# Modulation sums on TensorE in fewer, longer groups: a two-layer diffusion trunk on one core

## Chip, cores and metric

The kernel runs on one core of a Trainium2 chip. The metric is device time in microseconds (us): the median of several runs of the program. A lower number is better. The profile is one more execution of the same program, recorded by the hardware profiler.

## What is computed

A trunk of two layers works on 512 latent tokens and 256 context tokens of width 1024. Every layer normalises its input and modulates it: six rows of 1024 numbers (shift, scale and gate, for attention and for the MLP) come from a product of a conditioning vector with a 1024 x 6144 weight matrix. Latent tokens have the vector `c`, context tokens the vector `c_ctx`. Three attention groups (windowed, neighbourhood and latent) read one input projection; an output projection and a squared-ReLU MLP of width 4096 follow. The core of the reference:

```python
def modulate(h, shift, scale):
    return h * (1 + scale) + shift
...
    silu_c = jax.nn.silu(c)
    silu_cc = jax.nn.silu(c_ctx)
...
        mod_x = jnp.split((silu_c @ w_ada[l] + b_ada[l])[:, None, :], N_MOD, axis=-1)
        mod_c = jnp.split(silu_cc @ w_ada[l] + b_ada[l], N_MOD, axis=-1)
...
        hx = modulate(rmsnorm(x, norm1_g[l]), mod_x[0], mod_x[1])
        hc = modulate(rmsnorm(ctx, norm1_g[l]), mod_c[0], mod_c[1])
...
        x = x + mod_x[5] * sq_relu_mlp(modulate(rmsnorm(x, norm2_g[l]), mod_x[3], mod_x[4]),
...
```

Everything is in float32. The kernel keeps that accuracy in its large products by splitting each operand into a high and a low part and adding three products (high by high, low by high, high by low).

## The kernel before

**Work and staging.** The program is written as one pass over two layers: modulation, norm, input projection, attention groups B, A and C in turn, output projection, MLP. Weights come from memory in tiles of 128 x 1024 (tag `raw`, four buffers), and are split into `wh` and `wl` (L449 on ScalarE, L450 on VectorE). TensorE multiplies 128-row weight tiles with 384 or 512 token columns: L466 to L468 in the input projections, L603 and L652 to L661 in attention (scores, transposes, values), L693 to L695 in the output projection, L1075 to L1077 and L1109 to L1111 in the MLP. PSUM tiles have tags of their own: `psd` (two buffers), `pss` (three), `pst` (two), `psv` and `psa` (one each).

**What orders the work.** All engines run their own instruction list in order. Which list that is, the tile framework's scheduler decides when the program is built (`schedule_with_timeline_sim=True`): it simulates a timeline and, among the instructions that are ready, takes the one of highest priority, which by default is the one that stands earlier in the code. A block under `tc.high_priority()` stands ahead of all that. So the order on the engines differs from that of the code, and a change of priorities moves instructions in it.

**The modulation rows.** The first two rows of the first layer come in four quarters (`ada_quarter`), as the first thing in the program. Rows 2 to 4 of the first layer are made on TensorE while its attention runs (`ada_row`): eight blocks of 128 weight rows are loaded one by one (L209, on SP's queue, 512 KB each, to a `raw` tile), and each block has four matmuls (L211), one for each quarter of the 1024 features. The stationary operand is `ct`, 32 columns wide, so that the four quarters go to four column strips of the array (`tile_position`). They add up in the one `psa` tile:

```python
            for j in range(4):
                T.matmul(ps[32 * j:32 * j + 32, :256], ct[:, k, :], raw[:, j * 256:(j + 1) * 256],
                         start=(k == 0), stop=(k == KC - 1), tile_position=(0, 32 * j))
```

Row 5 of the first layer and all six of the second are made on VectorE while the MLP of the first layer holds TensorE (`ada_dve`, a generator that `step` in the MLP advances by one block at a time). For each block of weight rows (L269, 256 KB, tag `tm`) VectorE multiplies by the vector's entries and adds up (L275); an accumulator has 128 x 512 numbers, and there are four for a row (two halves of the features, two vectors), or two where the last layer needs only the latent vector. What is left is a sum over the 128 partitions: a matmul with a tile of ones for each accumulator, again 32 columns wide and on strips of their own (L280). Then, for a gate, VectorE adds the bias and the row goes to memory (L289 to L291); for a shift or a scale VectorE copies it (L297) and four transposes on TensorE (L300) bring it to columns.

**Names that follow.** Lines with a number, as L211, are those of the kernel before. A matmul in float32 is recorded as two passes, so that an "x2" in the trace's timeline is one matmul. The broad matmuls, whose operands are of the type fp32r, and the transposes are recorded as one pass. "Stop" below means a run of L211 or of L280 matmuls between two broad ones.

Of the kernel before, what the change touches and what calls it, by code (L numbers as in the profile page):

```python
# [26 lines left out]
RD = D ** -0.5  # exact: 1 / 32  # L27
# [3 lines left out]
STEPS = 2  # L31
STEP5 = 3
# [45 lines left out]
def hybrid_dit_kernel(  # L78
# [38 lines left out]
    def raw_tile(shape):  # L117
        return view(sbuf(1024, F32, "raw"), shape)
# [42 lines left out]
    def fence(t_, key):  # L161
        """holds the load of a tile back until another load of the start has come, so that the loads
        keep the order in which they are needed"""
        if FENCE.get(key, -1) in fences:
            V.tensor_copy(t_[:, 0:1], fences[FENCE[key]][:, 0:1])
# [24 lines left out]
    # silu of the two conditioning vectors (columns 0 and 1 of each chunk)  # L190
# [12 lines left out]
    def ada_row(l, m):  # L203
        """one of the six modulation rows of both conditioning vectors: column tile j holds
        the features j * 256 .. j * 256 + 255 on partitions 32 j (c) and 32 j + 1 (c_ctx)"""
        ps = ps_a()
        for k in range(KC):
            raw = raw_tile([D])
            nc.sync.dma_start(raw, w_ada[l, k * P:(k + 1) * P, m * D:(m + 1) * D])  # L209
            for j in range(4):  # L210
                T.matmul(ps[32 * j:32 * j + 32, :256], ct[:, k, :], raw[:, j * 256:(j + 1) * 256],  # L211
                         start=(k == 0), stop=(k == KC - 1), tile_position=(0, 32 * j))
# [22 lines left out]
    # the first shift and scale come by quarters of the features, to let the products start early  # L235
# [23 lines left out]
    def ada_dve(l, ms):  # L259
        """modulation rows on the vector engine, while the products hold the tensor engine;  # L260
        the sum over partitions is a product with ones"""
        for m in ms:
# [14 lines left out]
            # column tile j: the sums of half j % 2 for conditioning vector j // 2  # L277
            ps = ps_d()
            for j in range(2 * nw):
                T.matmul(ps[32 * j:32 * j + 32, :], ones, acc[j // 2][j % 2], start=True, stop=True,  # L280
                         tile_position=(0, 32 * j))
# [35 lines left out]
    def pump(n):  # L317
        """the first layer's rows are spread over its attention"""
        calls[0] += n
        if n and calls[0] in ADAPOS:  # L320
            pump_until(0, 2 + ADAPOS.index(calls[0]))
# [13 lines left out]
    # shift and 1+scale folded with the norm's gain, as per-partition columns  # L335
# [21 lines left out]
    def rstat_x(ss, n):  # L357
        """rows' halves of the mean square -> 1 / root of their sum + EPS"""
        r = small(n, "rst", 4)
        v_ = ss.rearrange("p (i h) -> p i h", h=2)  # L360
        V.scalar_tensor_tensor(r, v_[:, :, 0], EPS, v_[:, :, 1], ALU.add, ALU.add)
        G.tensor_tensor(r, r, mhalf[:, 0:n], ALU.pow)
        return r
# [25 lines left out]
    def norm_T(groups, l, which, pre=None):  # L389
        """normalised, modulated input, feature-major, as hi + lo"""  # L390
# [85 lines left out]
    def feat_pair(l, h, ws, ntoks):  # L476
        """two chunks at once, so that each feature block of the input is used as it comes"""
# [14 lines left out]
        else:  # L492
            # the first half of the tokens while the norm of the second is under way
# [18 lines left out]
    def rope(t_, rows, tab, mask):  # L512
        """in place on the latent tokens of a feature-major page"""
# [23 lines left out]
    def stack_q(t_, n):  # L537
        """two heads of a chunk -> per head one page holding hi and lo on its two halves"""
# [8 lines left out]
    def dup_k(t_, n):  # L547
        """two heads of a chunk -> per head (hi, hi) and (lo, lo)"""
# [35 lines left out]
    def att_unit(kind, rows, vap, put, sinkcols=None):  # L584
        """rows: four of dict(passes=[(lhsT, rhs)], segs=[(c0, n, mask)]), two per column half.
        vap(kb, half) -> values [128 keys, 64]; put(pv) stores the unit's output."""
# [42 lines left out]
        # key blocks: token tile -> column of the row's probabilities  # L629
# [85 lines left out]
    for l in range(DEPTH):  # L715
# [138 lines left out]
        # C: low-rank queries, keys/values and the shared rope key, token-major  # L854
# [37 lines left out]
        # the scores' scale goes with the gain of the query's norm  # L892
# [49 lines left out]
        def up_q(c):  # L942
            """one chunk of 128 features of the queries"""
# [12 lines left out]
        # the rope parts of all four heads  # L956
# [20 lines left out]
        def split_heads(res, n_all, rope_hl, name):  # L977
            """the two heads of a chunk to pages of 96 rows, 64 of the chunk and 32 of the rope part"""
# [249 lines left out]
def _layout(inp):  # L1228
# [15 lines left out]
    # relative position bias of a query in a 16-column block against the keys of three column blocks  # L1244
# [12 lines left out]
    def heads_apart(w, n):  # L1257
        """columns of the first n of every head, then those of the rest of every head"""
        w = w.reshape(L, w.shape[1], 4, -1)
        return np.concatenate([w[..., :n].reshape(L, w.shape[1], -1), w[..., n:].reshape(L, w.shape[1], -1)], axis=-1)  # L1260
# [29 lines left out]
```

## Time and profile before

| | us |
|---|---|
| the three runs | 1683.29, 1682.86, 1677.75 |
| their median | 1682.86 |
| span of the profiled execution | 1677.7 |
| TensorE (PE) busy in it, 8994 matmul passes | 1630.2 (97%) |
| VectorE (DVE) busy | 1012.7 (60%) |
| ScalarE (ACT) busy | 683.4 (41%) |
| GpSimd (POOL) busy | 606.3 (36%) |
| DMA queue of SP, share of 16 engines | 31.9% |
| mean granted TensorE clock | 0.990 |

The span runs from the first to the last instruction; the profiled execution is at the lower end of the three runs. Busy is the time in which an engine had an instruction in work; for TensorE that includes the time that matmuls overlap in its pipeline, so that a busy stretch can still hold time that another order of the same matmuls wouldn't need. The granted clock is a share of 2.4 GHz: 1.00 is that level, 0.50 the lower one of 1.2 GHz.

### The profile page before, as it was taken

What the parts mean: (1) busy time and instruction counts of PE and PEld (TensorE: products, weight loads), DVE (VectorE), ACT (ScalarE), POOL (GpSimd) and SP (SyncE); (2) the same over time, 40 slices, a digit from 0 to 9 for tenths busy, and PEclk for the clock granted to TensorE, in tenths of its full rate; (3) what the DMA queues carried; (4) which work ended last, traced back from release to release, by engine and by line L of the source; (5) the groups of instructions that cost most, each with busy time, mean ns of one, the idle gap of its engine ahead of it and who ended that gap; (6) DMA issues with size and microseconds to landing.
All of it is one profiled execution on the core that took longest, in us unless ns stands there. A gap on an engine that the chain in (4) does not pass through costs nothing.

```text
span 1677.7 us, 24080 instructions
## 1 busy us (share of the span) xinstructions
PE 1630.2 (97%) x8994; PEld 1354.9 (81%) x8994; DVE 1012.7 (60%) x1995; ACT 683.4 (41%) x1342; POOL 606.3 (36%) x564
## 2 busy tenths in 40 slices
PE   6999999999999999999999999999999899999997
PEld 3887788776798988889889879878776788888886
DVE  3555666687787667444454686686777633444346
ACT  5544466656631212212122245446755532222232
POOL 1111543553433342333424341144443323333335
PEclk8999999999999999999999999999999999999999
DMA  9545311220154423333333442222120233332332
GB/s 311 157 140 161 111 47 36 67 63 15 32 182 126 129 85 119 103 105 130 94 107 107 145 151 62 65 56 59 42 79 17 63 89 100 101 97 92 100 100 76
DMA packets 156421, 164.46 MB, mean 98 GB/s; under 512 B 8960, under 2 KB 111368, under 8 KB 156304
## 3 DMA queue, kind: packets, MB, share of 16 engines
q1 hardware_dynamic: 156304, 162.92, 31.9%
q8 instruction: 71, 1.16, 0.3%
q14 instruction: 46, 0.38, 0.1%
HBM read 155.53 MB, written 2.12 MB: 94 GB/s over the span
## 4 chain that ended last, share of the span: by engine, by line
PE 90%; DVE 5%; DMA 2%; ACT 1%; issue 1%; POOL 1%; SPq 0%; POOLq 0%; DVEq 0%; ACTq 0%
PE psd L1075 9%; PE psd L1076 9%; PE psd L1077 8%; PE psv L661 5%; PE pss L603 5%; PE pst L652 5%; PE pss L1109 3%; PE pss L1111 3%; PE pss L1110 3%; PE psd L466 3%; PE psd L468 3%; PE psd L467 3%; PE psa L1110 2%; PE psa L1111 2%; PE psd L693 2%; PE pst L1109 2%
## 5 line engine op out<-in xcount | busy, mean ns | idle before, releaser
L450 DVE TENSOR_TENSOR wl<-raw,wh 128x1024 fp32r<-128x1024 f32 (+1 forms) x168 | 220.7, 1315 | 197.6 <-issue 89.9
L712 POOL TENSOR_TENSOR xlat<-xlat,rtmp 128x512 f32<-128x512 f32 x159 | 236.1, 1509 | 280.7 <-DVE rtmp L711 273.6
L449 ACT CAST wh<-raw 128x1024 fp32r<-128x1024 f32 (+1 forms) x168 | 174.6, 1040 | 315.3 <-PE pst L1111 179.8
L1075 PE MATMUL psd<-hT,wh 128*128 128x384 f32 (+2 forms) x752 | 265.5, 353 | 3.9 <-DVE hT L413 3.9
L1076 PE MATMUL psd<-hT,wl 128*128 128x384 f32 (+2 forms) x752 | 264.9, 352 | 2.5 <-DVE wl L450 2.5
L1077 PE MATMUL psd<-hT,wh 128*128 128x384 f32 (+2 forms) x752 | 266.1, 354 | 0.2 <-POOL hT L415 0.2
L627 POOL TENSOR_TENSOR prob<-prob,sm 128x512 f32<-128x512 f32 (+3 forms) x110 | 126.4, 1157 | 258.5 <-DVE sm L620 211.8
L1084 POOL TENSOR_TENSOR relu<-relu 128x384 f32<-128x384 f32 (+1 forms) x96 | 98.2, 1024 | 319.2 <-ACT uh L1083 288.0
L1082 ACT ACTIVATE relu<-psd 128x384 f32<-128x384 f32 (+1 forms) x93 | 49.1, 528 | 283.7 <-PE psd L1077 280.6
L619 ACT ACTIVATE prob<-prob,m 128x513 f32<-128x513 f32 (+6 forms) x160 | 121.0, 756 | 99.2 <-DVE m L614 69.7
L1075 PEld LDWEIGHTS psd<-hT,wh 128*128 128x128 f32 x752 | 142.0, 189 | 15.8 <-DVE hT L413 4.4
L1076 PEld LDWEIGHTS psd<-hT,wl 128*128 128x128 f32 x752 | 141.9, 189 | 12.8 <-DVE wl L450 3.2
L1077 PEld LDWEIGHTS psd<-hT,wh 128*128 128x128 f32 x752 | 141.9, 189 | 10.9 <-issue 0.8
L1085 DVE TENSOR_TENSOR ul<-relu,uh 128x384 fp32r<-128x384 f32 (+1 forms) x96 | 59.1, 617 | 142.7 <-POOL relu L1084 142.6
L275 DVE SCALAR_TENSOR_TENSOR acc<-araw,consts,acc 128x512 f32<-128x512 f32 x140 | 114.3, 842 | 13.6 <-DMA araw<-in_w_ada_dram 12.9
L652 PEld LDWEIGHTS pst<-consts,prob 128*128 128x128 f32 x688 | 77.5, 140 | 49.6 <-issue 38.5
L652 PE MATMUL pst<-consts,prob 128*128 128x128 f32 x688 | 114.7, 282 | 2.3 <-POOL prob L627 1.3
L466 PE MATMUL psd<-hT,wh 128*128 128x384 f32 (+1 forms) x280 | 97.6, 349 | 0.5 <-DVE rtmp L711 0.2
L468 PE MATMUL psd<-hT,wl 128*128 128x384 f32 (+1 forms) x280 | 97.0, 346 | 1.1 <-DVE wl L450 1.1
L467 PE MATMUL psd<-hT,wh 128*128 128x384 f32 (+1 forms) x280 | 96.9, 346 | 0.0
L656 ACT COPY pT<-pst 128x512 f32<-128x512 f32 x124 | 70.9, 584 | 63.6 <-PE pst L652 63.3
L1111 PE MATMUL pss<-wh,ul 128*128 128x512 f32 x224 | 87.4, 390 | 0.0
(265 smaller groups left out, 3586.6 us busy)
## 6 DMA issues: line engine op xcount, KB each, us to landing
raw<-in_w_mlp_in_dram SPq DMA_DIRECT2D x64, 512.0 KB, 4.0
raw<-in_w_mlp_out_dram SPq DMA_DIRECT2D x64, 512.0 KB, 4.1
araw<-in_w_ada_dram SPq DMA_DIRECT2D x112, 256.0 KB, 4.7
raw<-in_w_in_dram SPq DMA_DIRECT2D x24, 512.0 KB, 4.2
raw<-in_w_ada_dram SPq DMA_DIRECT2D x24, 512.0 KB, 4.8
raw<-in_w_ada_dram SPq DMA_DIRECT2D x32, 256.0 KB, 5.6
raw<-in_w_out_dram SPq DMA_DIRECT2D x8, 512.0 KB, 5.5
raw<-in_w_out_dram SPq DMA_DIRECT2D x16, 256.0 KB, 3.5
```

Source lines behind the costliest of these rows:

```text
L449: A.copy(hi, raw)
L450: V.tensor_tensor(lo, raw, bc(hi), ALU.subtract)
L466: T.matmul(ps[:, :n], wh[:, k, :], hh[k][:, s0:s0 + n], start=(k == 0), stop=False)
L467: T.matmul(ps[:, :n], wh[:, k, :], hl[k][:, s0:s0 + n], start=False, stop=False)
L468: T.matmul(ps[:, :n], wl[:, k, :], hh[k][:, s0:s0 + n], start=False, stop=(k == KC - 1))
L627: G.tensor_tensor(p_[:, :w_], p_[:, :w_], sm.to_broadcast([P, w_]), ALU.mult)
L652: T.transpose(pt[:, r * P:(r + 1) * P], pts[r][:, pos[r][kb]:pos[r][kb] + P], ident)
L712: (V if fast and (RLAST if fast == "end" and t == 3 else RFAST)[dh] == "V" else G).tensor_tensor(xt[t][:, cs], xt[t][:, cs], tmp, ALU.add)
L1075: T.matmul(o_, wh[:, k, :], hh[k][:, sl], start=(k == 0), stop=False)
L1076: T.matmul(o_, wl[:, k, :], hh[k][:, sl], start=False, stop=False)
L1077: T.matmul(o_, wh[:, k, :], hl[k][:, sl], start=False, stop=(k == KC - 1))
L1111: T.matmul(a_, ul[:, ts_], wh[:, c % 2, :], start=False, stop=fin)
```

## The change

Two places are edited. In `ada_row` the loop takes the blocks of weight rows in pairs (`ADAB = 2`): both are loaded to `raw` tiles, and then the eight matmuls of the pair are issued together under high priority, those of the block loaded second first. The flags `start` and `stop`, which open and close the sum in PSUM, move with that order. In `ada_dve` the two or four sums of a row are issued under high priority too, in falling order of `j`. The number and the shapes of all instructions stay as they are. The other hunks of the diff take out comments and move line numbers by seven or eight: L211 becomes L218, L280 L288, L300 L308, L269 L276, L446 L454, L1075 to L1077 L1083 to L1085, L1109 to L1111 L1117 to L1119.

```diff
--- before.py
+++ after.py
@@ -24,11 +24,12 @@
 D_FF = 4096
 KC = D // P
 EPS = 1e-6
-RD = D ** -0.5  # exact: 1 / 32
+RD = D ** -0.5
 BIG = 1e30
 HUGE = 3e38
 PS = {"d": 2, "s": 3, "t": 2, "v": 1, "a": 1}
 STEPS = 2
+ADAB = 2
 STEP5 = 3
 PREP1 = 1
 PT = {"A": "A", "B": "AV", "C": "AV"}
@@ -201,15 +202,21 @@
     gdram = {}
 
     def ada_row(l, m):
-        """one of the six modulation rows of both conditioning vectors: column tile j holds
-        the features j * 256 .. j * 256 + 255 on partitions 32 j (c) and 32 j + 1 (c_ctx)"""
+
+
         ps = ps_a()
-        for k in range(KC):
-            raw = raw_tile([D])
-            nc.sync.dma_start(raw, w_ada[l, k * P:(k + 1) * P, m * D:(m + 1) * D])
-            for j in range(4):
-                T.matmul(ps[32 * j:32 * j + 32, :256], ct[:, k, :], raw[:, j * 256:(j + 1) * 256],
-                         start=(k == 0), stop=(k == KC - 1), tile_position=(0, 32 * j))
+        for k0 in range(0, KC, ADAB):
+            raws = []
+            for k in range(k0, k0 + ADAB):
+                raws.append(raw_tile([D]))
+                nc.sync.dma_start(raws[-1], w_ada[l, k * P:(k + 1) * P, m * D:(m + 1) * D])
+
+
+            with tc.high_priority():
+                for k in reversed(range(k0, k0 + ADAB)):
+                    for j in range(4):
+                        T.matmul(ps[32 * j:32 * j + 32, :256], ct[:, k, :], raws[k - k0][:, j * 256:(j + 1) * 256],
+                                 start=(k == ADAB - 1), stop=(k == KC - ADAB), tile_position=(0, 32 * j))
         if m in (2, 5):
             br = rtemp(256, name="brow")
             nc.sync.dma_start(br, brow[l, m])
@@ -274,11 +281,12 @@
                         else:
                             V.scalar_tensor_tensor(a_, raw, ct[:, k, w:w + 1], a_, ALU.mult, ALU.add)
                     yield
-            # column tile j: the sums of half j % 2 for conditioning vector j // 2
+
             ps = ps_d()
-            for j in range(2 * nw):
-                T.matmul(ps[32 * j:32 * j + 32, :], ones, acc[j // 2][j % 2], start=True, stop=True,
-                         tile_position=(0, 32 * j))
+            with tc.high_priority():
+                for j in reversed(range(2 * nw)):
+                    T.matmul(ps[32 * j:32 * j + 32, :], ones, acc[j // 2][j % 2], start=True, stop=True,
+                             tile_position=(0, 32 * j))
             rows = slice(0, 64 * nw)
             if m in (2, 5):
                 gd = dp.tile([2, D], F32, name=f"gate{l}_{m}")
```

The instruction lists differ on TensorE from the first layer's attention on, up to the end of its MLP; in the second layer they are the same after its first products. Three places show how.

In the attention of the first layer, within the second of `ada_row`'s three rows, TensorE's list of before reads (row number, line, operation, tile out<-in, shape of the moving operand, count; a modulation matmul shows as 32x256):

```order
548 L211 MATMUL psa<-raw,consts 32x256 x3
549 L661 MATMUL psv<-pT,vtok 64x256 x4
550 L652 MATMUL pst<-consts,prob 128x128 x4
551 L211 MATMUL psa<-raw,consts 32x256
552 L652 MATMUL pst<-consts,prob 128x128 x4
553 L603 MATMUL pss<-kh,qs 128x256
554 L603 MATMUL pss<-kl,qs 128x256
555 L571 MATMUL psd<-consts,qkraw 128x128
556 L211 MATMUL psa<-raw,consts 32x256 x3
557 L603 MATMUL pss<-kh,qs 128x256
558 L603 MATMUL pss<-kl,qs 128x256
559 L211 MATMUL psa<-raw,consts 32x256 x2
```

In the list of after a stop of the same modulation row reads:

```order
515 L476 MATMUL psd<-hT_126,wl 128x384
516 L474 MATMUL psd<-hT_128,wh 128x384
517 L475 MATMUL psd<-hT_129,wh 128x384
518 L476 MATMUL psd<-hT_128,wl 128x384
519 L474 MATMUL psd<-hT_130,wh 128x384
520 L218 MATMUL psa<-raw,consts 32x256 x8
521 L611 MATMUL pss<-kh,qs 128x256
522 L611 MATMUL pss<-kl,qs 128x256
523 L611 MATMUL pss<-kh,qs 128x256
```

Before, the matmuls of a block are taken apart by whatever was ready at the time, into stops of three, one, three and two. Now eight stand together, here between an input projection and scores.

In the first layer's MLP, the sums of the second layer's second row stand directly ahead of the four transposes of their result in the list of before (the first of the row's four sums stands alone, 66 rows further up):

```order
2839 L1109 MATMUL pst<-wh,uh 128x512
2840 L1110 MATMUL pst<-wl,uh 128x512
2841 L1111 MATMUL pst<-wh,ul 128x512
2842 L280 MATMUL psd<-acc,ones 32x512 x3
2843 L300 MATMUL psd<-consts,arow 128x128 x4
2844 L1075 MATMUL psd<-hT_4952,wh 128x384
2845 L1076 MATMUL psd<-hT_4952,wl 128x384
```

In the list of after the four sums stand 77 rows ahead of the transposes, within the products of another accumulation:

```order
2735 L1117 MATMUL pst<-wh,uh 128x512
2736 L288 MATMUL psd<-acc,ones 32x512 x4
2737 L1118 MATMUL pst<-wl,uh 128x512
2738 L1119 MATMUL pst<-wh,ul 128x512
2739 L1117 MATMUL pst<-wh,uh 128x512
...
2811 L1118 MATMUL pst<-wl,uh 128x512
2812 L1119 MATMUL pst<-wh,ul 128x512
2813 L308 MATMUL psd<-consts,arow 128x128 x4
2814 L1083 MATMUL psd<-hT_4952,wh 128x384
2815 L1084 MATMUL psd<-hT_4952,wl 128x384
```

Between those two places there are now 76 rows of MLP matmuls; before there were none.

On SP, whose list is its queue of loads, the end of the first layer's MLP read before (L446 from `w_in` are weights of the next input projections, L269 the weight rows for the modulation):

```order
186 L1122 DMA raw<-in_w_mlp_out_dram 128x2x512
187 L269 DMA araw<-in_w_ada_dram 128x512
188 L1122 DMA raw<-in_w_mlp_out_dram 128x2x512
189 L446 DMA raw<-in_w_in_dram 128x8x128 x5
190 L269 DMA araw<-in_w_ada_dram 128x512
191 L446 DMA raw<-in_w_in_dram 128x8x128
192 L269 DMA araw<-in_w_ada_dram 128x512 x15
193 L288 DMA arow<-in_b_ada_dram 32x512 x2
```

and reads now:

```order
183 L276 DMA araw<-in_w_ada_dram 128x512 x5
184 L1130 DMA raw<-in_w_mlp_out_dram 128x2x512 x2
185 L454 DMA raw<-in_w_in_dram 128x8x128 x3
186 L276 DMA araw<-in_w_ada_dram 128x512 x8
187 L454 DMA raw<-in_w_in_dram 128x8x128
188 L276 DMA araw<-in_w_ada_dram 128x512 x8
189 L454 DMA raw<-in_w_in_dram 128x8x128
190 L296 DMA arow<-in_b_ada_dram 32x512 x2
```

Of the last row's 16 modulation loads, one stood behind five of these weight loads and 15 behind six; they are now in two groups of eight behind three and four of them.

## Rows read from the trace of the kernel before

**Rows 1.** The page's part 4: the chain that ended last, by engine.

```profile
PE 90%; DVE 5%; DMA 2%; ACT 1%; issue 1%; POOL 1%; SPq 0%; POOLq 0%; DVEq 0%; ACTq 0%
```

**Rows 2.** Windows: stretch, length, busy PE PEld DVE ACT POOL, clock, DMA share, GB/s.

```profile
58.50:262.00 203.50, 202.56 (x1332) 162.01 (x1331) 131.66 (x369) 100.18 (x220) 60.83 (x81) 1.00 0.39 115
438.00:999.00 561.00, 557.39 (x2791) 493.33 (x2792) 335.07 (x446) 148.93 (x251) 207.41 (x165) 0.99 0.37 118
```

**Rows 3.** Timeline of TensorE, 75 us: start, length, line, [idle before <-releaser].

```profile
75.31 0.33 PE L467 MATMUL psd<-hT,wh 128*128 128x384 f32 x1
75.49 0.34 PE L468 MATMUL psd<-hT,wl 128*128 128x384 f32 x1
75.75 0.62 PE L211 MATMUL psa<-raw,consts 128*32 128x256 f32 x2
...
76.59 0.34 PE L467 MATMUL psd<-hT,wh 128*128 128x384 f32 x1
```

**Rows 4.** Timeline of TensorE, 67 us: six modulation matmuls in one stop.

```profile
67.20 0.34 PE L468 MATMUL psd<-hT,wl 128*128 128x384 f32 x1
67.47 1.06 PE L211 MATMUL psa<-raw,consts 128*32 128x256 f32 x12
...
68.68 0.28 PE L603 MATMUL pss<-kl,qs 128*128 128x256 f32 x1
```

**Rows 5.** Timeline of TensorE, 510 us: two sums in one stop.

```profile
510.11 0.34 PE L1076 MATMUL psd<-hT,wl 128*128 128x384 f32 x1
510.37 1.05 PE L280 MATMUL psd<-acc,ones 128*32 128x512 f32 x4
...
511.64 0.40 PE L1110 MATMUL pss<-wl,uh 128*128 128x512 f32 x1
```

**Rows 6.** Groups by line and shape, TensorE: passes | busy, mean ns | idle.

```profile
L211 PE MATMUL psa<-raw,consts 128*32 128x256 f32 x192 | 21.0, 390 | 0.4 <-DMA raw<-in_w_ada_dram 0.4
...
L280 PE MATMUL psd<-acc,ones 128*32 128x512 f32 x40 | 15.7, 605 | 0.0
```

**Rows 7.** Timeline at 686 us: TensorE and VectorE, three sums and their transposes.

```profile
685.66 1.06 PE L280 MATMUL psd<-acc,ones 128*32 128x512 f32 x6
685.70 2.32 DVE L450 TENSOR_TENSOR wl<-raw,wh 128x1024 fp32r<-128x1024 f32 x1
...
688.68 0.99 PE L300 MATMUL psd<-consts,arow 128*128 128x128 f32 x4 [1.95 <-DVE arow L297]
```

**Rows 8.** Windows, as in rows 2, of the stretch behind that.

```profile
688.70:692.30 3.60, 3.60 (x13) 3.60 (x14) 3.20 (x6) 0.00 (x0) 3.10 (x3) 0.53 0.70 245
```

**Rows 9.** Timeline of SP at 178 us: two loads of modulation weights.

```profile
178.08 0.34 SPq L209 DMA_DIRECT2D raw<-in_w_ada_dram  x1
...
178.53 0.37 SPq L209 DMA_DIRECT2D raw<-in_w_ada_dram  x1
```

**Rows 10.** Timeline of TensorE, 182 to 186 us: the stops that use them.

```profile
182.07 0.64 PE L211 MATMUL psa<-raw,consts 128*32 128x256 f32 x8 [0.16 <-DMA raw<-in_w_ada_dram]
...
184.49 0.64 PE L211 MATMUL psa<-raw,consts 128*32 128x256 f32 x8 [0.19 <-DMA raw<-in_w_ada_dram]
```

**Rows 11.** Line L209: its loads, from issue to landing.

```profile
DMA to landing us min/median/max: 3.6/4.8/6.7
```

**Rows 12.** Timeline of VectorE: accumulations and idle time of the last rows.

```profile
774.57 0.74 DVE L275 SCALAR_TENSOR_TENSOR acc<-araw,consts,acc 128x512 f32<-128x512 f32 x1
...
953.44 1.22 DVE L450 TENSOR_TENSOR wl<-raw,wh 128x1024 fp32r<-128x1024 f32 x1 [7.51 <-issue]
...
958.14 1.37 DVE L711 TENSOR_TENSOR rtmp<-pss,gates 128x512 f32<-128x512 f32 x2 [3.48 <-PE pss L1111]
...
985.51 0.73 DVE L275 SCALAR_TENSOR_TENSOR acc<-araw,consts,acc 128x512 f32<-128x512 f32 x1
```

**Rows 13.** Timeline of SP, 936 to 990 us: loads at the layer's end.

```profile
939.65 15.41 SPq L446 DMA_DIRECT2D raw<-in_w_in_dram  x5
...
964.23 8.65 SPq L269 DMA_DIRECT2D araw<-in_w_ada_dram  x15
```

## The prediction

> **What bounds the kernel now.** I read the page first: 90% of the chain that ended last is TensorE [rows 1]. Then the busy time by stage: in the first layer's attention (58.5 to 262 us) TensorE is busy for 202.6 of 203.5 us, in its MLP (438 to 999) for 557.4 of 561.0; no other engine passes 65% in either [rows 2]. So a step that TensorE doesn't have to make there is worth its whole length, and the word busy must be looked into: the timeline shows what it hides.
>
> Broad matmuls follow each other start to start in 0.18 us for 384 columns [rows 3], so about 0.12 for 256 columns, in proportion. A modulation matmul, which fills only 32 of the array's 128 columns, breaks that beat. One alone (x2, since each runs as two passes): from the broad matmul before it (75.49) to the second after it (76.59) are 1.10 us where two steps would be 0.36. The stop costs 0.74 us, of which 0.62 show as its own busy time and 0.12 as switching [rows 3]. Four of them, one block of weight rows, are busy for 0.64 (the x8 of [rows 10]): no longer than one. Six of them: 68.68 - 67.20 = 1.48, less 0.18 and 0.12, is 1.18 us, 1.06 of it busy [rows 4]. The price is that of a stop with one round of up to four matmuls, and some 0.43 more for a second round. The sums over partitions behave alike: two in one stop cost 511.64 - 510.11 = 1.53, less 0.36, is 1.17 us, 1.05 of it busy [rows 5].
>
> **The change, part by part.**
>
> *Modulation rows (L211).* The order of before has 30 such stops for 96 matmuls: 26 of one to four, three of five to seven, one of ten. Their busy time in sum is 21.0 us [rows 6]. The order of after has 12 stops of eight. Eight are two rounds, as six are: 1.06 us busy, 12.7 in sum, so 8.3 us less busy, and 18 switches of 0.12 fewer, 2.2. Together, 10.5, is the upper end; 8.3 is the lower, since eight of the old stops lie directly before a value product (L661), which is itself 64 columns wide and pays for a switch in any case. I take 9.0, nearer to the lower, because more than a quarter of the stops share their switch.
>
> *Sums (L280).* Before: 15 stops, 15.7 us busy [rows 6]. After: seven, three of four matmuls and four of two, each one round of 1.05 us: 7.4. Saved are 8.3 busy and eight switches of 0.12: 9.3 us. Three matmuls in one stop took 1.06 [rows 7], so a fourth adds next to nothing. The order of their four places is turned round, which no row shows; if turned places did not overlap, three stops would each take three passes of 0.43 more, 4 us in all, and if they overlap as before, nothing. I take nothing, which the rows in rising order are nearest to.
>
> *The stall at 686.7.* In the second layer's second row the last three sums are followed at once by the four transposes of their result (L300). These wait for VectorE, which first finishes a weight split of 2.32 us and then copies the result: TensorE idles 1.95 us [rows 7]. In the next 3.6 us the granted clock is 0.53, that is mostly the lower level, 1.2 GHz, and 13 matmuls fill it [rows 8]; nine at 0.18 and four narrower ones at 0.12 or less are some 2.0 us at 2.4 GHz, so 1.6 are lost. In the order of after these sums stand 77 rows ahead of their transposes, some 17 us of MLP matmuls, which cover split and copy. Saved 3.5 us; if that cover failed, nothing. No other stop of after has its transposes right behind it.
>
> *Added: waits for loads.* A stop of eight begins with the block that was loaded second, so it waits for both, and what stands behind it in TensorE's queue waits too. Mostly the weight tiles of the stop before are what comes free: in six of the nine follow-up stops both loads are issued after that stop (0.7 us after its start, the second 0.45 later), in three only one is. Before, loads issued at 178.08 and 178.53 [rows 9] were waited for until 182.07 and 184.49 [rows 10]: 4.0 and 6.0 us. So start to start 7.1 us are needed for two, 5 to 6 for one. The steps of the rows that the order of after puts between stops sum to 7.2, 7.7, 7.5, 5.8, 6.8 and 8.2 us for the six (the short ones in the third modulation row), and 6.1 to 6.2 for the three. Shortfall 1.3 + 0.3 = 1.6 us; none at the lower end, 8 at the upper (rival 1).
>
> The Trainium skill has a price for a load (DMA: Bandwidth & Descriptors, section Anatomy of one DMA): about 2.0 us fixed plus the bytes at 436 GB/s, fitted on another issue path than this kernel's. By it two blocks of 512 KB would take an estimated 4.4 us, no stop would wait, and the sum would be 1.6 us lower. The rows of this trace are longer, and I go by them.
>
> *Added: waits for sums.* Each of the seven stops now waits for all of VectorE's accumulations of its row. In five these ended before the time of the new place. In the second layer's third row the place was 774.9 us and the last accumulation ends at 775.3 [rows 12]: 0.5 us with its signal, taken. In its last row the order moves the stop 142 rows forward, to what was 971.3, while the accumulations ended at 986.2 [rows 12]. But it moves these as well: VectorE idled for 7.5 and 3.5 us before 953.4 and 958.1 [rows 12], because the loads of this row stood in SP's queue behind five weight loads issued over 15.4 us and came out only at 964.23 [rows 13]. After, eight of them stand behind three of those. Sixteen accumulations of 0.73 us fit into that idle time and the 8 us behind it. Cost 0, from -1 (a lighter VectorE at the layer's end) to 15, if the loads still come at 964.
>
> *Else.* The weight loads of the next projections follow the shorter modulation rows earlier on SP; the value products keep their 131 stops; the second layer's order is the same after its first products. All 0, and hidden behind a TensorE that has no gaps there.
>
> *Sum* against this execution's own 1677.7: - 9.0 - 9.3 - 3.5 + 1.6 + 0.5 = 1658.0. The three runs shown have their lowest at this time and their median at 1682.9, 5.2 above. A repeated measurement may fall on either level; by the other it is 1682.9 - 19.7 = 1663.2. I take about the middle, **1660 us**, against a median of 1682.9.
>
> **The rivals.**
> 1. *The loads come late.* If every block takes the 6.7 us of the slowest of this line [rows 11], the stops with two loads need 7.85 us (shortfalls 0.6, 0.2, 0.4, 2.0, 1.1: 4.3) and those with one 7.4 (1.3, 1.2, 1.3: 3.8). That is 8.1 us, and the one that idles 2 us pulls 1.6 of half clock behind it as in [rows 8]: 9.7, or 8 more than the sum has, 1668. For it: two loads side by side do slow each other. Against: the middle of this line is 4.8 [rows 11].
> 2. *Slower.* The same place, with longer loads: each stop that idles about 2 us costs 3.6 with the half clock after it. Nine are 32 us more than a sum without the 1.6: 1690. It is slower than before from seven such stops on, for which loads would have to take 8 us and more, beyond any seen here. The Trainium skill says of matmuls (TensorE: Matmul & The Clock Gate, section The mechanism) that they start and end strictly in order; by that rule nothing behind a waiting stop covers for it, and the trace agrees, with 0.16 and 0.19 us of idle ahead of such stops.
> 3. *The last row's sums come too early.* TensorE waits up to 15 us for them at the layer's end, and half clock follows: 1676. For it: VectorE idled while these loads were held back. Against: SP's queue is freed.
> 4. *The time goes into other waits.* A reordered attention stage gives back what it saved, where the softmax steps on VectorE and ScalarE pace it: 1680, no change. Against it: 0.9 us of idle in 203 [rows 2].
>
> **How the numbers follow.** Forecast 0.70 (1652 to 1667), rival 1 0.12, rival 3 0.05, rival 4 0.08, rival 2 0.05. A measurement of this kernel can tell about 0.3%, 5 us. Faster is below 1677.8, where forecast, rival 1 and rival 3 lie: 0.87; the same, rival 4: 0.08; slower 0.05. The low end takes the upper savings and no wait from the lower level (1654) and a lighter layer's end, 1652; the high end takes in rival 1 on the upper level, 1672.
>
> **What would show it.** Right: 12 modulation stops of x16 with about 1.06 us busy each, seven of sums; about 12.7 and 7.4 us busy in sum; full clock around the transposes of the second layer's second row; the first attention stage shorter by about 7 us, the MLP by about 12. Wrong: a load named before the modulation stops with several us, TensorE idle before the last sums, or another fall of the clock. All of it rests on a stop's price being the switch and not its matmuls: if four sums in one stop take 2 us, the second term falls.

## The result, and the profile after

The changed kernel takes 1664.45 us (median of four runs) beside 1682.38 for the kernel before: 17.9 us less. The ratio, taken over the runs and not from the medians, is 0.9899 with a 95% interval of 0.9879 to 0.9919, that is 17 us less (20 to 14). On another chip the two medians were 1664.70 and 1681.44, a ratio of 0.9902 (0.9886 to 0.9919). One of the four runs came out at 1998.74 us under a lower clock and is left out of the ratio. The forecast was 1660, the range 1652 to 1672.

The page of the changed kernel (part 1, then part 4 by engine) says little by itself. TensorE has 15.2 us less to do; it is busy for 97% of the span as before, and has 89% of the chain that ended last, against 90 [rows 1]:

```profile
PE 1615.0 (97%) x8994; PEld 1354.3 (81%) x8994; DVE 1010.4 (61%) x1995; ACT 684.2 (41%) x1342; POOL 610.5 (37%) x564
...
PE 89%; DVE 6%; DMA 2%; ACT 1%; issue 1%; POOL 0%; SPq 0%; POOLq 0%; DVEq 0%; ACTq 0%
```

The groups by line and shape answer to [rows 6]. The same 192 and 40 passes are busy for 12.8 and 7.4 us where they took 21.0 and 15.7; the waits for loads grew from 0.4 to 1.6:

```profile
L218 PE MATMUL psa<-raw,consts 128*32 128x256 f32 x192 | 12.8, 385 | 1.6 <-DMA raw<-in_w_ada_dram 1.6
...
L288 PE MATMUL psd<-acc,ones 128*32 128x512 f32 x40 | 7.4, 605 | 0.0
```

TensorE's timeline shows one stop of each kind (start, length, line). For the eight modulation matmuls, 141.44 - 139.95 less one step of 384 and one of 256 columns is 1.20 us, hardly more than the six of [rows 4]. For four sums, 657.93 - 656.28 less two steps of 512 columns (0.227 each) is 1.20 us, as for two in [rows 5]:

```profile
139.95 0.34 PE L474 MATMUL psd<-hT,wh 128*128 128x384 f32 x1
140.22 1.07 PE L218 MATMUL psa<-raw,consts 128*32 128x256 f32 x16
141.22 0.39 PE L611 MATMUL pss<-kh,qs 128*128 128x256 f32 x1
141.44 0.28 PE L611 MATMUL pss<-kl,qs 128*128 128x256 f32 x1
...
656.28 0.39 PE L1117 MATMUL pst<-wh,uh 128*128 128x512 f32 x1
656.60 1.06 PE L288 MATMUL psd<-acc,ones 128*32 128x512 f32 x8
657.60 0.50 PE L1118 MATMUL pst<-wl,uh 128*128 128x512 f32 x1
657.93 0.39 PE L1119 MATMUL pst<-wh,ul 128*128 128x512 f32 x1
```

Where the time went is read best from the starts of the same broad matmul in both timelines. The table is worked out from them: by how much the changed kernel is ahead, at a time of the kernel before.

| at (us of before) | ahead (us) | what lies in between |
|---|---|---|
| 60 | -0.6 | start of the program, not changed |
| 340 | 6.4 | modulation rows: +7 |
| 400 | 5.1 | half clock behind an idle time at 360 that is in both: -1.2 |
| 490 | 5.7 | clock at the start of the MLP: +0.6 |
| 600 | 10.4 | sums: four stops fewer by 1.18, +4.7 |
| 720 | 15.1 | one stop, the stall and the half clock at 688: +4.7 |
| 790 | 14.6 | one stop less, a new wait of 1.7: -0.5 |
| 1010 | 16.6 | two stops fewer by 1.18, small waits and transposes: +2.0 |
| 1300 and on | 15.3 | half clock near 1240, in both, of other cost: -1.3 |

Of the 19.7 us that the sum had, 15 are there in these two executions. The first attention stage is 7.0 us shorter and the MLP 10.9, where the prediction named about 7 and 12.

### The profile page after: what moved, and what is told of

Read it like the earlier page. It is cut to its first block, busy times and chain, and to the rows that moved or that the text cites. A ratio compares the mean times of both kernels' runs of the same rounds, so it can differ in the third digit from the quotient of the medians.

```text
span 1662.8 us, 24078 instructions
## 1 busy us (share of the span) xinstructions
PE 1615.0 (97%) x8994; PEld 1354.3 (81%) x8994; DVE 1010.4 (61%) x1995; ACT 684.2 (41%) x1342; POOL 610.5 (37%) x564
## 4 chain that ended last, share of the span: by engine, by line
PE 89%; DVE 6%; DMA 2%; ACT 1%; issue 1%; POOL 0%; SPq 0%; POOLq 0%; DVEq 0%; ACTq 0%
PE psd L1083 9%; PE psd L1084 9%; PE psd L1085 9%; PE psv L669 5%; PE pss L611 5%; PE pst L660 5%; PE pss L1117 3%; PE pss L1118 3%; PE pss L1119 3%; PE psd L474 3%; PE psd L475 3%; PE psd L476 3%; PE pst L1119 2%; PE pst L1118 2%; PE psv L1118 2%; PE psv L1119 2%
## 5 line engine op out<-in xcount | busy, mean ns | idle before, releaser
L457 ACT CAST wh<-raw 128x1024 fp32r<-128x1024 f32 (+1 forms) x168 | 174.8, 1041 | 301.1 <-PE pst L1119 175.4
L1083 PE MATMUL psd<-hT,wh 128*128 128x384 f32 (+2 forms) x752 | 264.8, 353 | 3.9 <-DVE hT L421 3.9
L1085 PE MATMUL psd<-hT,wh 128*128 128x384 f32 (+2 forms) x752 | 265.2, 353 | 0.1
L1090 ACT ACTIVATE relu<-psd 128x384 f32<-128x384 f32 (+1 forms) x93 | 49.1, 528 | 279.4 <-PE psd L1085 276.4
L1083 PEld LDWEIGHTS psd<-hT,wh 128*128 128x128 f32 x752 | 141.4, 188 | 15.7 <-DVE hT L421 4.4
L1084 PEld LDWEIGHTS psd<-hT,wl 128*128 128x128 f32 x752 | 141.4, 188 | 12.8 <-DVE wl L458 3.2
L1085 PEld LDWEIGHTS psd<-hT,wh 128*128 128x128 f32 x752 | 141.3, 188 | 9.7 <-DVE hT L423 0.3
L282 DVE SCALAR_TENSOR_TENSOR acc<-araw,consts,acc 128x512 f32<-128x512 f32 x140 | 116.9, 860 | 15.0 <-DMA araw<-in_w_ada_dram 14.0
L1118 PE MATMUL pss<-wl,uh 128*128 128x512 f32 x224 | 87.4, 390 | 0.0
```

What stands on the lines that cost most here:

```text
L457: A.copy(hi, raw)
L1083: T.matmul(o_, wh[:, k, :], hh[k][:, sl], start=(k == 0), stop=False)
L1084: T.matmul(o_, wl[:, k, :], hh[k][:, sl], start=False, stop=False)
L1085: T.matmul(o_, wh[:, k, :], hl[k][:, sl], start=False, stop=(k == KC - 1))
L1118: T.matmul(a_, uh[:, ts_], wl[:, c % 2, :], start=False, stop=False)
```

## Experiments

Line numbers are those of each run's own kernel: L287, L288 and L282 are the sums, L212, L217 and L218 the modulation matmuls. The kernel before had a median of 1682.38 us beside after; beside the runs below, made in three groups on three chips, it had 1680.31 (rows alone, sums alone, both loops rising, one strip after the other), 1679.56 (without priority, four blocks, quarters) and 1681.44 (the pair run together at the end). Ratios are to the kernel before of the same group, and a difference of 2 to 3 us between medians of two groups need not come from the edit.

**One part at a time.** Two kernels with one half of the diff each. The orders of TensorE divide cleanly: the first has the attention of after and the MLP of before, the second the reverse.

> Only the modulation rows (L218) are changed; the sums are issued as before. The order has 12 stops of eight modulation matmuls and the 15 sum stops of before, three of them directly ahead of their transposes. Theory (the price is paid per stop, and the two parts add up): about 7 us less than the kernel before, from the first layer's attention alone; the MLP of the first layer as long as before, with the idle time of about 2 us ahead of the transposes at 686 us still there. Rival (the gain comes from the sums alone, the waits of the pairs eat what the rows save): within 2 us of the kernel before.

> Only the sums (L280) are changed; the modulation rows are issued as before. The order has the 30 modulation stops of before and the seven sum stops of after. Theory: about 11 us less than the kernel before (8 stops by 1.18 us are 9.4, the idle time of 2.0 and the half clock of 1.6 behind it, less 1.7 for six MLP matmuls that now come ahead of their weight split, and 0.3 for transposes in two places), all of it between 500 and 1000 us. Rival (the idle time goes elsewhere, only stops are saved): about 8 us.

Rows alone: 1673.0 us, 0.9962 of before (0.9949 to 0.9975). Sums alone: 1671.96, 0.9953 (0.9941 to 0.9965). The two gains by medians, 7.3 and 8.4, add up to 15.7, close to the 16.7 and 17.9 of both. The 8.4 alone would fit the rival of sums alone (8) about as well as the theory (11); what speaks for the theory is the timeline. The groups by line show each gain in its own place, first rows alone, then sums alone:

```profile
L287 PE MATMUL psd<-acc,ones 128*32 128x512 f32 x40 | 15.7, 605 | 0.0
L218 PE MATMUL psa<-raw,consts 128*32 128x256 f32 x192 | 12.8, 385 | 1.6 <-DMA raw<-in_w_ada_dram 1.6
```

```profile
L212 PE MATMUL psa<-raw,consts 128*32 128x256 f32 x192 | 21.0, 390 | 0.6 <-DMA raw<-in_w_ada_dram 0.5
L282 PE MATMUL psd<-acc,ones 128*32 128x512 f32 x40 | 7.4, 605 | 0.0
```

With sums alone the run is 10.9 us ahead of before at 1010 us, as expected, and 8.6 at the end: two stretches of half clock in the second layer, whose order is the same, took the rest. With rows alone the stall ahead of the transposes is still there, but the clock does not fall behind it. The timeline row and the window (columns as in [rows 2]) of rows alone stand against [rows 7, 8]:

```profile
681.27 0.66 PE L307 MATMUL psd<-consts,arow 128*128 128x128 f32 x4 [1.95 <-DVE arow L304]
...
682.00:685.60 3.60, 3.60 (x23) 3.60 (x22) 2.51 (x5) 0.00 (x0) 2.42 (x2) 1.00 0.80 275
```

**What makes the stops long: the direction of the loops or the priority.** First the loops of after count up:

```diff
-                for k in reversed(range(k0, k0 + ADAB)):
+                for k in range(k0, k0 + ADAB):
...
-                                 start=(k == ADAB - 1), stop=(k == KC - ADAB), tile_position=(0, 32 * j))
+                                 start=(k == 0), stop=(k == KC - 1), tile_position=(0, 32 * j))
...
-                for j in reversed(range(2 * nw)):
+                for j in range(2 * nw):
```

> After, with both loops counting up instead of down (block loaded first, j = 0 first), still under high priority and with both loads ahead. The order now has 24 modulation stops of four and 17 sum stops, 14 of them of one matmul. Theory (the falling order is what makes the stops long, since all of a group then wait for the last operand; the price is per stop): rows 24 by 0.74 = 17.8 instead of 12 by 1.20 = 14.4 us, less 1.9 of waits for loads; sums 10 more stops by 1.18 = 11.8 us; in all 13 us slower than after, about 1677. Rival (high priority or the pairs of loads bring the gain, the direction of the loops doesn't matter): within 2 us of after, 1664.

1679.55 us, 0.9997 of before (0.9987 to 1.0007): the whole gain is gone, with the priority and the paired loads still in place. Only the cover of the stall stays: TensorE has no idle time ahead of L308. Its groups:

```profile
L288 PE MATMUL psd<-acc,ones 128*32 128x512 f32 x40 | 17.8, 605 | 0.0
L218 PE MATMUL psa<-raw,consts 128*32 128x256 f32 x192 | 15.3, 391 | 3.8 <-DMA raw<-in_w_ada_dram 3.8
```

Sums that may run at once, run at once: each starts when its own accumulator is done, and makes a stop of its own. With the last accumulator first, all of them wait for it. The rows were busy for 2.5 us more than in after, and their waits grew by 2.2 us where I had expected them to vanish.

Then the priority is taken away, from the sums alone and from the modulation matmuls alone; pairs and falling order stay:

```diff
-            with tc.high_priority():
-                for j in reversed(range(2 * nw)):
-                    T.matmul(ps[32 * j:32 * j + 32, :], ones, acc[j // 2][j % 2], start=True, stop=True,
-                             tile_position=(0, 32 * j))
+            for j in reversed(range(2 * nw)):
+                T.matmul(ps[32 * j:32 * j + 32, :], ones, acc[j // 2][j % 2], start=True, stop=True,
+                         tile_position=(0, 32 * j))
```

> After, with the high priority taken from the sums alone; they are still issued in falling order of j. The order has nine sum stops instead of seven, and in the second layer's second row three sums stand directly ahead of their transposes again, as before the change. Theory (the falling order groups the sums; the priority adds two stops fewer and the cover of the stall): 2 stops by 1.18 and an idle time of 2.0 us back, 4.4 us slower than after (about 1669), or 6 if half clock follows the idle time as it did in the profiled run of before. Rival (the priority is what gains): 10 us or more slower than after.

> After, with the high priority taken from the modulation matmuls alone; pairs of loads and falling order stay. The order has 21 modulation stops (11 of one to four matmuls, 9 of five to eight, one of eleven) instead of 12. Theory (price per stop by the matmuls on one column strip): 11 by 0.74, 9 by 1.19 and 1.6 are 20.4 us instead of 14.4, less up to 1.9 us of waits for loads: 4 to 6 us slower than after, about 1669. Rival (the two loads ahead are what gains, for instance through earlier loads): within 2 us of after.

Sums without priority: 1672.04 us, 0.9952 of before (0.9938 to 0.9965), 7.6 and 7.3 us above the two medians of after (1664.45 and 1664.70), where 4.4 to 6 were expected. The nine stops are busy for 9.5 us, and the stall is back, longer than before, with half clock behind it (681.1 to 684.5 us). In TensorE's timeline:

```profile
676.72 1.06 PE L287 MATMUL psd<-acc,ones 128*32 128x512 f32 x6
680.32 0.66 PE L307 MATMUL psd<-consts,arow 128*128 128x128 f32 x4 [2.54 <-DVE arow L304]
```

Against the profile of after this execution is 2.0 us late from its start already, and has one more fall of the clock in the second layer. In its MLP, where the edit is, it loses 6.8 us against after. The stop count accounts for 2.4 of these and the stall with its half clock for 4.1. The rest of the difference between the medians stays open; they are from different chips.

Rows without priority: 1670.68 us, 0.9944 (0.9930 to 0.9959), 6 us above after, where 4 to 6 were expected. The 6.0 that the price per stop asks for are there: 21 stops are busy for 18.8 us in place of 12.8. But the waits, which I expected to shrink by up to 1.9 us, grew by 2.1. One pair waits 2.5 us, with 3.4 us of half clock behind it, and the timeline loses 8.1 us against after in this stage. So the 6 us between the medians fit the expectation partly by luck. The group of this run:

```profile
L217 PE MATMUL psa<-raw,consts 128*32 128x256 f32 x192 | 18.8, 407 | 3.7 <-DMA raw<-in_w_ada_dram 3.7
```

**What a stop costs.** Three kernels change what is inside it. In the first the two blocks of one quarter follow each other directly, on one column strip:

```diff
-                for k in reversed(range(k0, k0 + ADAB)):
-                    for j in range(4):
+                for j in range(4):
+                    for k in reversed(range(k0, k0 + ADAB)):
```

> After, with the eight modulation matmuls of a stop in another order: both blocks of one quarter of the features directly after each other, so that neighbours use the same column strip. Still 12 stops of eight, the same result. Theory (four matmuls on four strips run side by side, two on one strip after each other, and all start in order): five rounds instead of two, 3 by 0.43 us more for each stop, 15 us in all, about 1680, and about 2.3 us busy for a stop instead of 1.06. Rival (the price of a stop is the switch alone, the matmuls in it cost what their columns cost): within 2 us of after.

1664.47 us, 0.9906 (0.9893 to 0.9919), the same as after. My theory failed here. The stop of this kernel in TensorE's timeline is 1.09 us busy, not 2.3:

```profile
134.87 0.34 PE L474 MATMUL psd<-hT,wh 128*128 128x384 f32 x1
135.14 1.09 PE L218 MATMUL psa<-raw,consts 128*32 128x256 f32 x16
136.16 0.44 PE L475 MATMUL psd<-hT,wh 128*128 128x384 f32 x1
```

The single passes inside it start in four groups of four, 0.24, 0.216 and 0.216 us apart, as in after. Within a group the starts are 13 ns apart, where they are 7 ns apart in after: the sign in the trace that the matmuls did come in another order. In this order a strict start one after the other would leave the second strip empty until the first has begun its last pass. So here a strip that is busy did not hold up a matmul for another strip behind it. What counts in these runs is how many passes the fullest strip has.

In the second, four blocks make a stop (`ADAB = 4`):

> After, with four blocks of weight rows to a stop instead of two: six stops of sixteen modulation matmuls, and all four weight buffers wanted at once. Theory of the price: 0.31 and 0.216 for each of the eight passes on a strip, some 2.05 us for a stop, 12.3 in sum instead of 14.4. Theory of the loads: the second stop of a row comes 9 to 43 rows (2 to 8 us) after the first, and four loads that start when the first stop frees the buffers take 6 us or more: about 10 us of waits instead of 1.9; in all 5 to 8 us slower than after, about 1671. Rival (loads are hidden as well as with two): 2 us faster than after.

1668.84 us, 0.9930 (0.9915 to 0.9945), with runs from 1664.2 to 1670.8. The timeline shows a stop of sixteen matmuls without a wait, and the one with the long wait:

```profile
97.53 0.33 PE L475 MATMUL psd<-hT,wh 128*128 128x384 f32 x1
97.80 1.93 PE L218 MATMUL psa<-raw,consts 128*32 128x256 f32 x32
99.66 0.44 PE L669 MATMUL psv<-pT,vtok 128*64 128x128 f32 x4
...
155.13 1.93 PE L218 MATMUL psa<-raw,consts 128*32 128x256 f32 x32 [3.39 <-DMA raw<-in_w_ada_dram]
```

Six by 1.93 are 11.6 us busy: the price was right (eight passes by 0.216 and the ends). The waits were not: 3.4 us in one place, where I had expected 10. The stops save 1.2 us of busy time against after, and the waits take 1.8 more. That is not all of the 4 us between the medians: the profiled run is only 1.9 longer than that of after, so the rest stays open (the runs spread over 6.7 us).

In the third, the sums of the four rows with one vector use all four strips, half as many columns each:

```diff
-                for j in reversed(range(2 * nw)):
-                    T.matmul(ps[32 * j:32 * j + 32, :], ones, acc[j // 2][j % 2], start=True, stop=True,
+                for j in reversed(range(4)):
+                    T.matmul(ps[32 * j:32 * j + 32, :256], ones, acc[0][j // 2][:, (j % 2) * 256:(j % 2) * 256 + 256],
+                             start=True, stop=True, tile_position=(0, 32 * j))
...
-                for q in range(4):
-                    T.transpose(pt[:, q * P:q * P + 64 * nw], ar[rows, q * P:(q + 1) * P], ident[rows, rows])
+                for q in range(2):
+                    T.transpose(pt[:, q * P:(q + 1) * P], ar[:, q * P:(q + 1) * P], ident)
```

> After, with the sums of the four rows that need only the latent vector split over all four column strips: four matmuls of 256 columns in place of two of 512, the same sums; their result then needs two transposes of 128 x 128 in place of four of 64 x 64. Theory (a stop lasts as long as the passes on its fullest strip): 1.18 becomes 0.74 for four stops, 1.8 us, and the transposes fit the array without a switch, about 1 us: 2.8 us faster than after, about 1661.6. Rival (a stop's price is a fixed switch): the stops stay at 1.18 and the time within 1 us of after.

1661.26 us, 0.9890 (0.9876 to 0.9904). The group and one stop of it in the timeline:

```profile
L289 PE MATMUL psd<-acc,ones 128*32 128x256 f32 x32 | 2.6, 391 | 0.9 <-DVE acc L282 0.9
```

```profile
850.36 0.39 PE L1147 MATMUL pst<-wl,uh 128*128 128x512 f32 x1
850.68 0.64 PE L289 MATMUL psd<-acc,ones 128*32 128x256 f32 x8
851.25 0.50 PE L1148 MATMUL pst<-wh,ul 128*128 128x512 f32 x1
851.59 0.39 PE L1146 MATMUL pst<-wh,uh 128*128 128x512 f32 x1
```

851.59 - 850.36 less two steps of 0.227 is 0.78 us for a stop that took 1.18. One of the four gives 0.9 back as a wait for the accumulations. To compare with after on one chip, both were run again together:

> The version with quarters once more, unchanged, beside the changed kernel on the same chip. Theory: 2 to 3 us less than the changed kernel's median, near 1661.5, with the four small stops near 0.77 us again. Rival (the 3 us between the two medians came from different chips and clocks): within 1 us of the changed kernel.

> The changed kernel once more, unchanged, beside the version with quarters on the same chip: 1664 to 1665.

1662.22 us (0.9883 of before, 0.9865 to 0.9900) beside 1664.70 (0.9902, 0.9886 to 0.9919). The intervals overlap; the medians differ by 2.5 us this time and by 3.2 before. In the timelines the MLP, where the edit is, is shorter by 1.3 and 1.7 us: four stops by 0.4, about 1 for the transposes by what is left over, less the wait for the accumulations (1.3 and 0.9). The other 1 to 1.5 us between the medians stay open. It has the lowest medians of all versions tried.

**Does half clock belong to an idle time?** Both kernels once more, unchanged, for one more profiled execution each.

> The kernel before once more, unchanged, to see whether the half clock belongs to a place of the program. Theory (a fall of the clock follows some of the idle times of 1 to 2 us and not others, from execution to execution): the idle time of 2.0 us ahead of the transposes at 687 us is there again, but the 3.4 us of half clock behind it need not be, and a fall may come near 366 or 1120 us, where the first profile had none. Rival (the fall belongs to the idle time): the same falls near 689 and none near 366 and 1120.

> The changed kernel once more, unchanged. Theory: the same idle times (1.3 us at 359, 1.5 at 760, 2 in the second layer), with falls of the clock behind another choice of them; spans differ from 1662.8 by 1.2 us for each fall more or fewer. Rival: the same falls, near 361, 433 and 1235 us, and a span within 0.3 us.

Spans of 1678.7 and 1663.8 us. In the kernel before the half clock behind the stall came again (0.54 in 689.8 to 693.4 us), and apart from the start of the program no other place changed, against what I had expected of it. In the changed kernel the one near 361 us did not come again. One fall fewer should have made it 1.2 us shorter; it was 1.0 longer, through its start (0.7) and longer waits for loads and sums. The idle time ahead of it is in these four executions, and in the one beside the quarters too; in the timelines of before and of after:

```profile
365.85 0.44 PE L652 MATMUL pst<-consts,prob 128*128 128x128 f32 x2 [1.31 <-POOL prob L627]
```

```profile
359.51 0.44 PE L660 MATMUL pst<-consts,prob 128*128 128x128 f32 x2 [1.34 <-POOL prob L635]
```

The windows behind it, of before, of after, and of after once more (the last but two columns: the granted clock):

```profile
365.90:369.30 3.40, 3.40 (x21) 2.64 (x21) 3.31 (x14) 2.82 (x7) 2.74 (x2) 1.00 0.01 2
```

```profile
361.00:364.40 3.40, 3.40 (x15) 3.11 (x15) 3.12 (x14) 2.12 (x5) 2.24 (x2) 0.50 0.01 2
```

```profile
360.30:363.70 3.40, 2.64 (x16) 2.14 (x17) 3.26 (x14) 2.95 (x6) 3.40 (x3) 1.00 0.00 0
```

Neither side is borne out whole. Behind the idle time of 1.3 us the clock fell in one of the three kept executions of after and in neither of the two of before, at one and the same place of the program; the fall behind the stall came in three of the four executions that had the stall.

## Why the prediction held, point by point

*Price of a stop.* Right, by switch and rounds. Summed over all modulation stops, each from the broad matmul ahead to the second behind less their own steps, the rows cost 23.7 us before and 16.4 after. Without the waits for loads in them (0.7 and 1.9) these are 23.0 and 14.5: 8.5 us saved, between the 8.3 and the 9.0. The rounds have to be read as passes on one strip; the order inside a stop, which I left at nothing for the sums, costs nothing in the directions tried, but it decides whether there is a stop of four at all (rising).

*Sums.* 17.8 us before and 8.3 after by the same count: 9.5, where the term was 9.3.

*The stall.* Its cover holds: no idle time ahead of L308, and full clock there, in TensorE's timeline of after:

```profile
674.96 0.39 PE L1119 MATMUL pst<-wh,ul 128*128 128x512 f32 x1
675.20 0.60 PE L308 MATMUL psd<-consts,arow 128*128 128x128 f32 x4
```

The 2.0 us of idle time are saved in every kept execution of after; the 1.6 of half clock only where it would have come, as the run with rows alone shows.

*Waits for loads.* 1.2 us more than before, where the term was 1.6, but not in its places: that the two numbers are near is luck. None of the nine follow-up stops, from which the term was worked out, waits in this execution; the first stops of the second and the third row do, in TensorE's timeline:

```profile
117.99 1.07 PE L218 MATMUL psa<-raw,consts 128*32 128x256 f32 x16 [0.42 <-DMA raw<-in_w_ada_dram]
...
178.95 1.07 PE L218 MATMUL psa<-raw,consts 128*32 128x256 f32 x16 [1.14 <-DMA raw<-in_w_ada_dram]
```

After once more had 2.4 us of such waits, one of them ahead of a follow-up stop:

```profile
187.12 1.07 PE L218 MATMUL psa<-raw,consts 128*32 128x256 f32 x16 [0.65 <-DMA raw<-in_w_ada_dram]
```

Why the list has these stops ahead of their loads is not shown. The priority alone is not the reason: without it the waits of the pairs were longer (3.7 us). The loads themselves were faster than I took them to be, 3.9 us in the median, against 4.8 [rows 11] (line L212 of after):

```profile
DMA to landing us min/median/max: 3.7/3.9/5.7
```

So the loads issued in pairs were here not slower than those of before, against what was said for rival 1. By the price of the Trainium skill (DMA: Bandwidth & Descriptors, section Anatomy of one DMA), an estimated 4.4 us for two such loads, no follow-up stop would wait; in this execution none did, and the price lies between that median and the slowest, 5.7.

*Waits for sums.* None in this execution, in the third row neither. After once more waits 0.6 us for the last row's sums:

```profile
956.18 1.05 PE L288 MATMUL psd<-acc,ones 128*32 128x512 f32 x4 [0.63 <-DVE acc L282]
```

So this place is just covered, and rival 3, with up to 15 us, did not happen. Rivals 1, 2 and 4 did not either: the waits for loads were 1.6 and 2.4 us, and the attention stage kept its 7.0. One sign of being wrong did show, another fall of the clock (361 us), but not in every execution.

*Everything else at 0.* This is the step that failed. In the list of after six MLP matmuls (L1117) of the third row's stretch stand 24 rows further up, ahead of a whole chunk of L1083 to L1085. Their weights are not yet split there, and the copy L457 that makes them waits in ScalarE's list behind an L1090, which waits for TensorE. Timelines of TensorE and ScalarE:

```profile
758.10 0.34 PE L1085 MATMUL psd<-hT,wh 128*128 128x384 f32 x1
759.95 0.73 PE L1117 MATMUL pss<-wh,uh 128*128 128x512 f32 x2 [1.51 <-ACT wh L457]
```

```profile
758.47 0.49 ACT L1090 ACTIVATE relu<-psd 128x384 f32<-128x384 f32 x1 [3.11 <-PE psd L1085]
758.86 1.04 ACT L457 CAST wh<-raw 128x1024 fp32r<-128x1024 f32 x1
```

It costs 1.7 us. The idle time of 1.5 us is in all ten kept executions with falling sums, and in none of the other four (before twice, rows alone, both loops rising). The order showed it; I had looked at the sums' rows and not at what moved past them. The narrow transposes of one row, which now stand in two places, cost 0.3 more.

*From the sum to the time.* 19.7 less 1.7 and 0.3 are 17.7. By the medians it is 17 to 18. Between the two profiles only 15 were found. Most of the rest is half clock in places that the change does not touch (1.2 at 360 us, 1.3 net near 1240, less 0.6 at 438); 0.6 is lost at the start of the program, where the clock is not the reason, since it was the execution of before that had 13.7 us of half clock there.

The forecast of 1660 was lower than sum and median give (1663.2), because it took the middle of two levels. That was a misreading. A profile's span is some 1.8 us shorter than the device time of the same execution (1662.8 and 1664.70 for after, 1678.7 and 1680.48 for before once more), so the span of 1677.7 belongs to about 1679.5 (an estimate) and not to the lowest run. And there are no two levels: the 41 runs of before on record lie between 1677.7 and 1684.2 us with no gap wider than 0.5. The low end of the range, 1652, is one us below what its own terms give (1654 less 1).

## What to carry to other kernels

In this kernel a narrow matmul between broad ones is priced by the stop: the switch and the passes on its fullest column strip, not by the count of matmuls. So gather them, spread them over all strips, and where a scheduler starts everything as soon as it can, issue the one with the latest operand first. After such a regrouping read the whole list of the waiting engine, not only the rows that were meant to move.

## What the hardware did that I had not expected

Matmuls on different column strips did not wait for each other: sixteen passes issued strip by strip, four in a row for each, ran in 1.09 us, sixteen in turn in 1.07. The Trainium skill says of matmuls that they start strictly in order (TensorE: Matmul & The Clock Gate, section The mechanism); across strips this run differs. And the same idle time of 1.3 us was followed by full clock in two executions of a kernel and by 3.4 us at 1.2 GHz in a third.
